# Gate tables of a product-key expert layer from bf16 one-hots, with the gate in three exact bf16 parts

## The chip, the cores and the metric

The kernel runs on one core of a Trainium2 chip. The metric is the device time of one execution in microseconds. Of the kernel before, three timed executions are at hand, and one more that was profiled.

## The reference

One layer of a streaming encoder on 512 tokens of width 2048, in f32: a mixer of two attention branches, then a PEER layer (retrieval of single-neuron experts by product keys), then a norm. Only the PEER layer matters here:

```python
scores = jnp.einsum('thpc,hpnc->thpn', q, sub_keys)        # 8 heads, 2 halves, 128 keys each
s1, i1 = lax.top_k(scores[:, :, 0], 16)
s2, i2 = lax.top_k(scores[:, :, 1], 16)
cand_score = s1[..., :, None] + s2[..., None, :]           # 256 candidates a head
cand_id = i1[..., :, None] * 128 + i2[..., None, :]
top_score, pos = lax.top_k(cand_score, 16)                 # over the 256
gates = jax.nn.softmax(top_score, axis=-1)
act = gelu(einsum('thkd,td->thk', expert_u[ids], x))
out = einsum('thk,thkd->td', gates * act, expert_v[ids])
```

Each token picks 8 x 16 = 128 of 16,384 experts. An expert's number is a pair (a, b) of two indices from 0 to 127.

## The kernel before

For the first 352 tokens the kernel doesn't gather experts. It multiplies with all 16,384 of them and weighs the result by a **gate table**: for each token a matrix of 128 x 128, which holds the gates at the 128 chosen pairs (a, b) and zero elsewhere. The other 160 tokens are served by gathering rows of the expert matrices.

The work on the PEER layer stands in this order in the program:

- *Selection* (`choose`): queries, scores, and top 16 by instructions of VectorE. It leaves three tiles: `ia` and `ib`, the two indices of each pick, and `gt`, its gate, all f32, with tokens on partitions.
- *Tables* (lines 766 to 793): `ia`, `ib` and `gt` are transposed by TensorE (`pstr`) and copied back by ScalarE, so that the 128 picks stand on the partitions and the tokens along the row. Then 22 blocks (`tb`) of 16 tokens follow, each in four groups of four tokens, 88 groups in all. VectorE makes one-hots for a group: one `tensor_tensor` compares `ib`, held for 128 elements, with the numbers 0 to 127 (`i128`) for four tokens at once, 512 elements (line 782, tile `ab`). Four `tensor_scalar` instructions, one for each token, compare `ia` with them and multiply by the gate (line 787). TensorE multiplies the two one-hots of a token, which sums over the 128 picks and gives the token's table in PSUM (`psgt`, line 789), ScalarE copies the four tables to `st` (line 790), and GpSimd's queue stores a block's tables to memory (`gsp`, line 791).
- *Weighted products* (`weigh` and after): 128 groups of experts, each with its up-projection (`psu`), the table's factors loaded from `gsp`, and the down-projection (`psy`).

`early` puts up-projections (`expert_up`) between the steps of selection and tables, one for two blocks of three. Such an up-projection is 48 products of 128 x 352 on TensorE (`psu`, lines 116 to 118), whose weights are loaded in two halves (`wr`), rounded by ScalarE (`wh`, line 108) and completed by VectorE (`wl`, line 109), and an activation (`gl`, line 536 on VectorE, 539 on ScalarE). `pace` puts gathers between them: GpSimd fetches 128 rows (`row`, line 561) and VectorE multiplies and sums 2048 elements (line 568).

Products with f32 operands (`psgt`) are single instructions that the trace shows as two records. The up- and down-projections use f32 values split into two parts of a type that TensorE takes in one pass.

Every engine works off its queue in order. The order within a queue is made by a scheduler that reorders what the program lists, by its own costs and by the data that instructions wait for. Each tag of a pool has a fixed number of buffers: `ab` two for each of the one-hots, `pg` (PSUM, `psgt`) two, `st` two, `wh` and `wl` three each.

## Time and profile before

| | us |
|---|---|
| median of three runs | 3785.46 |
| lowest and highest | 3780.77, 3790.85 |
| the profiled execution | 3782.03 |
| its span, from the first to the last instruction | 3780.3 |

The profiled execution has 1.7 us around its span. The tables are made from 1909 to 2118 us of the span. The page gives shares of busy time over the whole span; the windows view gives them for a stretch; the view of groups sums instructions of one line and shape; the timeline has single instructions with their start and duration. Instructions of one engine that follow each other overlap a little, so that the distance between starts is shorter than the duration.

### The profile page before, as it was taken

Reading aid. Unit: us, or ns where it says so; the run is one execution under the profiler, and the core shown is the slowest. Engines: PE = TensorE matmul, PEld = TensorE weight load, DVE = VectorE, ACT = ScalarE, POOL = GpSimd, SP = SyncE. Lnnn points to the kernel's source line nnn. Section 1 sums busy time; section 2 is a strip of 40 time slices with the busy share of each in tenths; the row PEclk is TensorE's granted clock in tenths of the full one; section 3 lists DMA queues with packets and bytes.
Section 4 is the critical chain, followed back from the end, with each engine's and each line's share of the span. In section 5 each row is a group of like instructions: output and inputs, shape, how many; then the busy total and the mean of one; then the engine's idle time right before and its main releaser. Section 6 shows DMA issues by size and latency. Waiting matters only on the chain.

```text
span 3780.3 us, 52236 instructions
## 1 busy us (share of the span) xinstructions
PE 3676.0 (97%) x20745; PEld 3384.4 (90%) x20745; DVE 2640.2 (70%) x4067; ACT 1291.3 (34%) x1808; POOL 515.2 (14%) x432
## 2 busy tenths in 40 slices
PE   8999999999999999999999898999999999999997
PEld 7888888888887878799999798999999999999997
DVE  5333445444555346799699888988888888888885
ACT  4334222232223223344355332333333333333333
POOL 0000000000000000011211122222222222222220
PEclk9999999999999999999999999999999999999999
DMA  4222222222224233376867899998999989999983
GB/s 141 80 78 77 98 95 95 89 87 84 85 95 138 95 100 101 128 267 251 294 229 264 288 336 333 352 334 326 333 336 348 345 324 349 340 343 344 332 306 112
DMA packets 233701, 827.26 MB, mean 219 GB/s; under 512 B 21736, under 2 KB 82664, under 8 KB 189680
## 3 DMA queue, kind: packets, MB, share of 16 engines
q1 hardware_dynamic: 174032, 450.30, 34.5%
q0 software_dynamic: 49920, 360.74, 24.8%
q10 hardware_dynamic: 9504, 12.88, 0.9%
q8 instruction: 163, 2.67, 0.3%
q14 instruction: 82, 0.67, 0.1%
HBM read 784.72 MB, written 39.11 MB: 218 GB/s over the span
## 4 chain that ended last, share of the span: by engine, by line
PE 81%; DVE 9%; DMA 5%; issue 3%; ACT 1%; SPq 0%; POOL 0%; DVEq 0%; POOLq 0%; ACTq 0%
PE psy L118 7%; PE psy L117 7%; PE psy L116 7%; PE psu L118 6%; PE psu L116 6%; PE psu L117 6%; PE psg L118 3%; PE psg L117 3%; PE psq L118 3%; PE psg L116 3%; PE psq L117 3%; PE psq L116 3%; DVE wl L109 2%; DVE ab L787 2%; PE psk L118 2%
## 5 line engine op out<-in xcount | busy, mean ns | idle before, releaser
L108 ACT ACTIVATE wh<-wr 128x1024 fp32r<-128x1024 f32 x768 | 813.6, 1061 | 1933.4 <-PE psy L117 581.0
L109 DVE TENSOR_TENSOR wl<-wr,wh 128x1024 fp32r<-128x1024 f32 x768 | 935.5, 1221 | 504.4 <-ACT wh L108 500.5
L116 PE MATMUL psy<-wg,wh 128*128 128x352 f32 x2048 | 668.6, 327 | 26.6 <-ACT wg L820 25.8
L117 PE MATMUL psy<-wg,wh 128*128 128x352 f32 x2048 | 672.0, 328 | 8.7 <-DVE wg L821 8.7
L118 PE MATMUL psu<-h,wl 128*128 128x352 f32 x2048 | 666.7, 326 | 12.8 <-DVE wl L109 12.5
L118 PE MATMUL psy<-wg,wl 128*128 128x352 f32 x2048 | 669.8, 328 | 8.4 <-DVE wl L109 8.3
L116 PE MATMUL psu<-h,wh 128*128 128x352 f32 x2048 | 666.6, 325 | 4.0 <-DVE gl L536 2.9
L117 PE MATMUL psu<-h,wh 128*128 128x352 f32 x2048 | 662.8, 324 | 0.0
L116 PEld LDWEIGHTS psy<-wg,wh 128*128 128x128 f32 x2048 | 391.1, 191 | 29.0 <-ACT wg L820 27.6
L118 PEld LDWEIGHTS psu<-h,wl 128*128 128x128 f32 x2048 | 385.5, 188 | 18.9 <-DVE wl L109 18.7
L117 PEld LDWEIGHTS psy<-wg,wh 128*128 128x128 f32 x2048 | 391.0, 191 | 11.0 <-DVE wg L821 10.9
L118 PEld LDWEIGHTS psy<-wg,wl 128*128 128x128 f32 x2048 | 391.0, 191 | 10.0 <-DVE wl L109 9.9
L116 PEld LDWEIGHTS psu<-h,wh 128*128 128x128 f32 x2048 | 386.6, 189 | 5.0 <-issue 3.2
L117 PEld LDWEIGHTS psu<-h,wh 128*128 128x128 f32 x2048 | 386.9, 189 | 0.0
L561 POOL DMA_INDIRECT row<-eu,idx x128 | 192.4, 1503 | 901.5 <-DVE row L568 606.4
L568 DVE SCALAR_TENSOR_TENSOR row<-row,rstd_t,h2g 128x2048 f32<-128x2048 f32 x128 | 300.1, 2345 | 6.5 <-DMA row<-eu,idx 6.5
L586 DVE SCALAR_TENSOR_TENSOR acc<-row,gact,acc 128x2048 f32<-128x2048 f32 x128 | 300.1, 2345 | 1.9 <-DMA row<-ev,idx 1.9
L561 POOL DMA_INDIRECT row<-ev,idx x128 | 182.2, 1424 | 508.0 <-DVE acc L586 478.1
L116 PE MATMUL psq<-h,wh 128*128 128x512 f32 x512 | 204.5, 399 | 8.8 <-ACT wh L108 8.8
L117 PE MATMUL psq<-h,wh 128*128 128x512 f32 x512 | 205.6, 401 | 1.5 <-DVE h L167 1.4
L118 PE MATMUL psq<-h,wl 128*128 128x512 f32 x512 | 204.6, 400 | 0.1
L118 PE MATMUL psg<-h,wl 128*128 128x512 f32 x512 | 203.3, 397 | 0.0
(311 smaller groups left out, 5513.7 us busy)
## 6 DMA issues: line engine op xcount, KB each, us to landing
wr<-uT SPq DMA_DIRECT2D x256, 512.0 KB
wr<-vP SPq DMA_DIRECT2D x256, 512.0 KB
wr<-w_qk SPq DMA_DIRECT2D x64, 512.0 KB
wr<-w_g SPq DMA_DIRECT2D x64, 512.0 KB
gsp<-st POOLq DMA_DIRECT2D x22, 1024.0 KB
wr<-w_br SPq DMA_DIRECT2D x32, 512.0 KB
wr<-w_o SPq DMA_DIRECT2D x32, 512.0 KB
wr<-w_q SPq DMA_DIRECT2D x32, 512.0 KB
```

The source lines that it names most:

```text
L108: nc.scalar.activation(hi, raw, AF.Copy)
L109: ins = nc.vector.tensor_tensor(lo, raw, hi.bitcast(F32), op=ALU.subtract)
L116: nc.tensor.matmul(ps, wh, ah, start=start, stop=False)
L117: nc.tensor.matmul(ps, wh, al, start=False, stop=False)
L118: nc.tensor.matmul(ps, wl, ah, start=False, stop=stop)
L561: nc.gpsimd.indirect_dma_start(out=row.rearrange("p k q -> p (k q)"), out_offset=None, in_=table, in_offset=bass.IndirectOffsetOnAxis(ap=i ...
L568: nc.vector.scalar_tensor_tensor(row, row, rstd_t[:, NT - 1:NT], h2g, op0=ALU.mult, op1=ALU.mult, accum_out=gact[:, i:i + 1])
L586: nc.vector.scalar_tensor_tensor(accg, row, gact[:, i:i + 1], accg, op0=ALU.mult, op1=ALU.add)
L787: nc.vector.tensor_scalar(ab[0][:, i], i128, tr[0][:, t:t + 1], tr[2][:, t:t + 1], op0=ALU.is_equal, op1=ALU.mult)
```

## The change

`ia` and `ib` become the halves of one tile, `iab`. After the transposes they are written as bf16, into the start of the same tile (`tid`; numbers up to 127 are exact in bf16). The gate is taken apart: its bf16 rounding, the bf16 rounding of the rest, and what then is left, each exact in bf16 (`tg`, three casts and two subtractions on VectorE).

For a group of four tokens one `tensor_tensor` makes the one-hots of both indices, 2 x 4 x 128 elements in bf16 (`eq`), and another multiplies the first index's one-hots by the three parts of the gate, 3 x 4 x 128 elements in bf16 (`ga`). TensorE then makes three bf16 products for a token, summed in PSUM. In the selection stage the two position tiles and the row of numbers that they are compared with become bf16 as well.

```diff
-        ia = s1p.tile([P, NT, HK], F32, name="ia")
-        ib = s1p.tile([P, NT, HK], F32, name="ib")
+        iab = s1p.tile([P, 2, NT, HK], F32, name="iab")
+        ia, ib = iab[:, 0], iab[:, 1]
...
-        i128 = s1p.tile([P, NK], F32, name="i128")
+        i128 = s1p.tile([P, NK], BF16, name="i128")
...
+            pa16, pb16 = small(BF16, "b0h"), small(BF16, "b2h")
-            nc.vector.tensor_tensor(pa_, pa_, pc_, op=ALU.add)
+            nc.vector.tensor_tensor(pa16, pa_, pc_, op=ALU.add)
...
+        packed = iab.rearrange("p n t q -> p (n t q)").bitcast(BF16)[:, :5 * ND * P].rearrange("p (n q) -> p n q", n=5)
+        tid, tg = packed[:, :2], packed[:, 2:]
         for n, src in enumerate((ia, ib, gt)):
             ps = psx.tile([P, ND, P], F32, tag="psx", name="pstr")
             for t in range(ND):
                 nc.tensor.transpose(ps[:, t], src[:, t], ident)
-            nc.scalar.activation(src[:, :ND], ps, AF.Copy)
-            tr.append(src.rearrange("p t q -> p (t q)"))
+            nc.scalar.activation((tid[:, n] if n < 2 else src[:, :ND].rearrange("p t q -> p (t q)")),
+                                 ps.rearrange("p t q -> p (t q)"), AF.Copy)
+        rest = gt[:, :ND].rearrange("p t q -> p (t q)")
+        for m in range(3):
+            nc.vector.tensor_copy(tg[:, m], rest)
+            if m < 2:
+                nc.vector.tensor_tensor(rest, rest, tg[:, m], op=ALU.subtract)
...
-                ab = [se.tile([P, 4, NK], F32, tag=f"ab{i}", bufs=2, name="ab") for i in range(2)]
-                nc.vector.tensor_tensor(ab[1], i128.unsqueeze(1).to_broadcast([P, 4, NK]),
-                                        tr[1][:, tk].unsqueeze(2).to_broadcast([P, 4, NK]), op=ALU.is_equal)
+                eq = se.tile([P, 2, 4, NK], BF16, tag="eq", bufs=2, name="eq2")
+                nc.vector.tensor_tensor(eq, i128.unsqueeze(1).unsqueeze(1).to_broadcast([P, 2, 4, NK]),
+                                        tid[:, :, tk].unsqueeze(3).to_broadcast([P, 2, 4, NK]), op=ALU.is_equal)
+                ga = se.tile([P, 3, 4, NK], BF16, tag="ga", bufs=2, name="ga")
+                nc.vector.tensor_tensor(ga, eq[:, 0].unsqueeze(1).to_broadcast([P, 3, 4, NK]),
+                                        tg[:, :, tk].unsqueeze(3).to_broadcast([P, 3, 4, NK]), op=ALU.mult)
                 ps = pg.tile([P, 4, NK], F32, tag="pg", name="psgt")
                 for i in range(4):
-                    t = tb * TB + t4 + i
-                    nc.vector.tensor_scalar(ab[0][:, i], i128, tr[0][:, t:t + 1], tr[2][:, t:t + 1], op0=ALU.is_equal,
-                                            op1=ALU.mult)
-                    nc.tensor.matmul(ps[:, i], ab[0][:, i], ab[1][:, i], start=True, stop=True)
+                    for m in range(3):
+                        nc.tensor.matmul(ps[:, i], ga[:, m, i], eq[:, 1, i], start=m == 0, stop=m == 2)
```

On VectorE's queue the first groups stand so in the kernel before (`ab` are the one-hots, `row` a gathered row, `gl` an up-projection's activation):

```order
L536 TENSOR_TENSOR gl<-psu,rstd 128x352
L568 SCALAR_TENSOR_TENSOR row,gact<-row,rstd_t,h2g 128x2048
L782 TENSOR_TENSOR ab<-i_9669,ib 128x512
L787 TENSOR_SCALAR ab<-i_9669,ia,gt 128x128 x4
L782 TENSOR_TENSOR ab<-i_9669,ib 128x512
L787 TENSOR_SCALAR ab<-i_9669,ia,gt 128x128 x4
```

And so in the changed kernel, from the parts of the gate on:

```order
L782 TENSOR_TENSOR gt<-gt,iab 128x384
L536 TENSOR_TENSOR gl<-psu,rstd 128x352
L780 CAST iab<-gt 128x384
L109 TENSOR_TENSOR wl<-wr,wh 128x1024
L791 TENSOR_TENSOR ga<-eq_15124,iab 128x1536
L791 TENSOR_TENSOR ga<-eq_15142,iab 128x1536
L788 TENSOR_TENSOR eq_15160<-i_9668,iab 128x1024
L788 TENSOR_TENSOR eq_15178<-i_9668,iab 128x1024
L791 TENSOR_TENSOR ga<-eq_15160,iab 128x1536
L791 TENSOR_TENSOR ga<-eq_15178,iab 128x1536
```

Two groups now go together, both comparisons and then both products, where before a group was finished before the next one began; the subtraction and cast of the gate's parts stand ahead of the first product, with a weight split between.

On TensorE's queue, where the tables begin, before (`psgt` are the tables, `psu` an up-projection):

```order
L789 MATMUL psgt<-ab 128x128 x4
L116 MATMUL psu<-h_8494,wh 128x352
L117 MATMUL psu<-h_8494,wh 128x352
L118 MATMUL psu<-h_8494,wl 128x352
L116 MATMUL psu<-h_8494,wh 128x352
L789 MATMUL psgt<-ab 128x128 x4
L117 MATMUL psu<-h_8494,wh 128x352
L118 MATMUL psu<-h_8494,wl 128x352
L116 MATMUL psu<-h_8494,wh 128x352
L117 MATMUL psu<-h_8494,wh 128x352
L789 MATMUL psgt<-ab 128x128 x2
```

And in the changed kernel, at the end of the first group's twelve products (each with its own load of weights, which the order now lists):

```order
L796 LDWEIGHTS ga
L796 MATMUL psgt<-eq_15124,ga 128x128
L117 MATMUL psu<-h_8494,wh 128x352
L118 MATMUL psu<-h_8494,wl 128x352
L116 MATMUL psu<-h_8494,wh 128x352
L117 MATMUL psu<-h_8494,wh 128x352
L118 MATMUL psu<-h_8494,wl 128x352
L116 MATMUL psu<-h_8494,wh 128x352
L796 LDWEIGHTS ga
L796 MATMUL psgt<-eq_15142,ga 128x128
```

A token's one product became three, and the up-projections moved: before, 654 of their products stand between the first and the last table, in 36 places four of them in a row and in two places 46; now 593 stand there, eight times 46 and six times 22 in a row, and up to ten groups of tables follow each other with none between. From the transposes to the down-projection it is 665 in both.

On SyncE's queue the weight loads keep their order; at the end of the stage the first load of the tables stands one weight load earlier. On GpSimd's queue the stores of tables and the gathers stand in a slightly different order.

## Rows read from the trace of the kernel before

**Rows 1.** The page, busy us (share of the span) and instructions of each engine.

```profile
PE 3676.0 (97%) x20745; PEld 3384.4 (90%) x20745; DVE 2640.2 (70%) x4067; ACT 1291.3 (34%) x1808; POOL 515.2 (14%) x432
```

**Rows 2.** Windows: stretch, its length, busy us by engine, granted clock, DMA share, GB/s.

```profile
1909.00:2118.00 209.00, 195.55 (x1371) 188.41 (x1369) 208.44 (x507) 122.72 (x131) 26.86 (x33) 0.99 0.71 258
2118.00:2129.10 11.10, 0.08 (x1) 0.00 (x0) 0.05 (x1) 1.02 (x1) 1.53 (x2) 0.65 0.87 310
```

**Rows 3.** The chain of waits, 1850 to 2220 us: start, us, what.

```profile
2026.27 1.03 DVE ab L787 x4
...
2119.43 5.83 DMA gsp<-st
2125.38 3.65 DMA h<-gsp
```

**Rows 4.** Groups, 1909.5 to 2118 us: count, busy us, mean ns, idle before.

```profile
L789 PE MATMUL psgt<-ab 128*128 128x128 f32 x704 | 98.6, 283 | 7.7 <-DVE ab L787 7.3 <-issue 0.5
L787 DVE TENSOR_SCALAR ab<-i,ia,gt 128x128 f32<-128x128 f32 x352 | 97.7, 343 | 0.0
...
L782 DVE TENSOR_TENSOR ab<-i,ib 128x512 f32<-128x512 f32 x88 | 60.2, 684 | 0.0
...
L109 DVE TENSOR_TENSOR wl<-wr,wh 128x1024 fp32r<-128x1024 f32 x29 | 35.0, 1216 | 0.0
...
L568 DVE SCALAR_TENSOR_TENSOR row<-row,rstd_t,h2g 128x2048 f32<-128x2048 f32 x12 | 28.1, 2344 | 0.0
...
L536 DVE TENSOR_TENSOR gl<-psu,rstd 128x352 f32<-128x352 f32 x14 | 7.3, 520 | 0.3 <-PE psu L118 0.2
```

**Rows 5.** Waits, 1909.5 to 2118 us: us in total, times, longest us.

```profile
PE psgt L789 <- DVE ab L787: 7.3, 11, 2.1
```

**Rows 6.** Timeline of VectorE, two places: start, us, engine, line, tiles.

```profile
1909.58 0.69 DVE L782 TENSOR_TENSOR ab<-i,ib 128x512 f32<-128x512 f32 x1
1910.19 1.11 DVE L787 TENSOR_SCALAR ab<-i,ia,gt 128x128 f32<-128x128 f32 x4
1911.21 0.68 DVE L782 TENSOR_TENSOR ab<-i,ib 128x512 f32<-128x512 f32 x1
...
1930.69 2.34 DVE L568 SCALAR_TENSOR_TENSOR row<-row,rstd_t,h2g 128x2048 f32<-128x2048 f32 x1
...
1932.96 1.21 DVE L109 TENSOR_TENSOR wl<-wr,wh 128x1024 fp32r<-128x1024 f32 x1
1934.10 0.68 DVE L782 TENSOR_TENSOR ab<-i,ib 128x512 f32<-128x512 f32 x1
```

**Rows 7.** Groups of VectorE in the selection stage, 1380 to 1900 us.

```profile
L700 DVE TENSOR_TENSOR eq<-b,i 128x512 bf16<-128x512 f32 x32 | 20.8, 683 | 0.0
...
L704 DVE TENSOR_TENSOR eq<-eq,f 128x512 bf16<-128x512 bf16 x32 | 12.4, 414 | 0.0
...
L705 DVE TENSOR_REDUCE ib<-eq 128x32 f32<-128x512 bf16 x16 | 10.7, 672 | 0.0
...
L748 DVE COPY spread<-ident 128x128 f32<-128x128 f32 x1 | 0.2, 218 | 0.0
```

**Rows 8.** Timeline of TensorE, 1954 to 1962 us.

```profile
1955.72 0.32 PE L118 MATMUL psu<-h,wl 128*128 128x352 f32 x1
1955.88 1.95 PE L789 MATMUL psgt<-ab 128*128 128x128 f32 x16
1957.58 0.41 PE L118 MATMUL psu<-h,wl 128*128 128x352 f32 x1
```

**Rows 9.** Windows of 4 us behind the last tables; the clock stands ahead of DMA's share.

```profile
2108.00:2112.00 4.00, 4.00 (x31) 4.00 (x31) 3.85 (x5) 1.56 (x3) 0.00 (x0) 1.00 0.94 362
...
2124.00:2128.00 4.00, 0.00 (x0) 0.00 (x0) 0.00 (x0) 0.00 (x0) 0.00 (x0) 0.50 0.91 330
...
2132.00:2136.00 4.00, 4.00 (x18) 4.00 (x18) 3.03 (x7) 1.99 (x4) 0.00 (x0) 0.61 0.65 190
2136.00:2140.00 4.00, 3.15 (x19) 2.77 (x19) 1.86 (x4) 1.03 (x2) 0.00 (x0) 1.00 0.51 151
```

More of the change, by code (lines that the diff above doesn't have):

```diff
@@ L633, in block_kernel @@
         pg = pool("pg", 2, space=PSUM, cm=s1)
-        ia = s1p.tile([P, NT, HK], F32, name="ia")
-        ib = s1p.tile([P, NT, HK], F32, name="ib")
+        iab = s1p.tile([P, 2, NT, HK], F32, name="iab")
+        ia, ib = iab[:, 0], iab[:, 1]
         gt = s1p.tile([P, NT, HK], F32, name="gt")
-        i16 = s1p.tile([P, TOPK], F32, name="i16")
+        i16 = s1p.tile([P, TOPK], BF16, name="i16")
         nc.gpsimd.iota(i16, pattern=[[1, TOPK]], base=0, channel_multiplier=0, allow_small_or_imprecise_dtypes=True)
-        i128 = s1p.tile([P, NK], F32, name="i128")
+        i128 = s1p.tile([P, NK], BF16, name="i128")
         nc.gpsimd.iota(i128, pattern=[[1, NK]], base=0, channel_multiplier=0, allow_small_or_imprecise_dtypes=True)
@@ L694, in choose @@
             nc.vector.tensor_tensor(pc_, pc_, lt, op=ALU.mult)
-            nc.vector.tensor_tensor(pa_, pa_, pc_, op=ALU.add)
+            pa16, pb16 = small(BF16, "b0h"), small(BF16, "b2h")
+            nc.vector.tensor_tensor(pa16, pa_, pc_, op=ALU.add)
             nc.vector.tensor_tensor(pd_, pd_, lt, op=ALU.mult)
-            nc.vector.tensor_tensor(pb_, pb_, pd_, op=ALU.subtract)
-            for (uf, f, dst) in ((pa_, ids[0], ia), (pb_, ids[1], ib)):
+            nc.vector.tensor_tensor(pb16, pb_, pd_, op=ALU.subtract)
+            for (uf, f, dst) in ((pa16, ids[0], ia), (pb16, ids[1], ib)):
                 eq = se.tile([P, n * TOPK, TOPK], BF16, tag="ab0", name="eq")
@@ L765, in block_kernel @@
             early(UPS, pace)
-        tr = []
+        s2.close()
+        se = pool("scat", 2, cm=s1)
+        packed = iab.rearrange("p n t q -> p (n t q)").bitcast(BF16)[:, :5 * ND * P].rearrange("p (n q) -> p n q", n=5)
+        tid, tg = packed[:, :2], packed[:, 2:]
         for n, src in enumerate((ia, ib, gt)):
@@ L771, in block_kernel @@
                 nc.tensor.transpose(ps[:, t], src[:, t], ident)
-            nc.scalar.activation(src[:, :ND], ps, AF.Copy)
-            tr.append(src.rearrange("p t q -> p (t q)"))
-        s2.close()
-        se = pool("scat", 2, cm=s1)
+            nc.scalar.activation((tid[:, n] if n < 2 else src[:, :ND].rearrange("p t q -> p (t q)")),
[5 more added lines that the diff above has]
+                nc.vector.tensor_tensor(rest, rest, tg[:, m], op=ALU.subtract)
         for tb in range(TD // TB):
```

## The prediction

> **What bounds the kernel now.** I read the page's busy shares first: TensorE is busy for 97% of the span [rows 1], so at first sight only TensorE work is worth taking out. The change, though, lies in one stage, and a stage has to be read alone. The windows view of that stage, 1909 to 2118 us, turns the picture round: VectorE is busy 208.44 of 209.00 us and TensorE 195.55 [rows 2]. The chain of waits agrees: inside the stage its pieces are the VectorE instructions of the table builder (`ab`), with the splits of weights (`wl`) and the gathered rows between them [rows 3]. TensorE waits there for the one-hots, 7.3 us in all in 11 places [rows 5]; VectorE waits for practically nobody. So what this stage is worth is read from VectorE, and TensorE time taken out of it is worth nothing as long as VectorE stays the longer of the two.
>
> The stage is a sum of VectorE steps, where a step is the distance from one start to the next (shorter than a duration, since neighbours overlap). A group of four tokens is one comparison of 512 elements, 0.61 us, and four scalar instructions, 1.02 us: 1.63 us [rows 6]. 88 groups make 143 us. Beside them run 29 weight splits of 1024 elements at 1.14 us, 12 gathered rows of 2048 at 2.27 us [rows 4, 6], and 14 activations of 352 elements, for which I estimate 0.45 us: 33 + 27 + 6 us. Together 210 us, against 208.44 us read. The sum closes, so it may be used for the changed kernel.
>
> **What the change takes out of VectorE's queue and puts in.** Out go 88 comparisons and 352 scalar instructions. In come 88 comparisons of 1024 elements (both indices at once) and 88 products of 1536 elements (three parts of the gate). The changed kernel thus has two instructions instead of five in a group, but each token now has 256 + 384 = 640 elements written by two-operand instructions instead of 128 by such and 128 by scalar ones. The question is at what rate they run.
>
> The step of a two-operand instruction is proportional to its elements: 0.61 us at 512, 1.14 at 1024, 2.27 at 2048 [rows 6], about 1.1 ns an element plus some 0.07 us, with every operand f32. I call this the single rate. At it the new comparison takes 1.14 us and the new product, halfway between 1.14 and 2.27, 1.70 us: 2.84 us a group, 1.21 us more than now.
>
> The new instructions have only bf16 operands, and the trace has one such two-operand instruction: the product in the selection stage, 414 ns for 512 elements, where the comparison ahead of it with f32 inputs takes 683 [rows 7]. The 269 ns between them are half of 512 elements' time. At that doubled rate the steps would be 0.60 and 0.87 us, 1.47 us a group, 0.16 us less than now. These are the two ends, and they have different signs.
>
> I take the slow end, for the shape of the operands. In the fast row all operands run on from element to element; its repeated factor is repeated by whole rows of 16. Both new instructions have one operand that stands still within a row: one index, or one part of a gate, is held for 128 elements. The rows nearest in this respect are the comparison that the change removes, and the bf16-writing comparison of the selection stage, 683 ns, in which an index is held for 16 elements: both at the single rate, though with f32 inputs [rows 4, 7]. That bf16 operands alone don't double a rate is shown by the reduction, 672 ns for 512 bf16 elements [rows 7]. No row has the held operand and bf16 together.
>
> Here the Trainium skill speaks against the change. Its "Vector Engine (DVE) Microarchitecture Reference", section 5.1 Performance modes, says that the paired 2-byte rate asks for a step of one element in every input and output, and that a two-source instruction with 2-byte operands which reads one element 16 times over was tried on trn2 and ran at the single rate, while a whole row read again and again kept the double one. No row here shows the first case; the second agrees with the 414 ns. By this page the sum is that of the slow end; by its "VectorE: DVE Perf Modes", tier table, read without the condition, a bf16 `tensor_tensor` gets the double rate, and the sum would be that of the fast end.
>
> So: 88 x 1.21 = **+106.5 us**, all on the path, since VectorE is what the stage waits for. At 1.675 us for the product (512 and 1024 drawn on) it would be 104.
>
> **The split of the gate.** Three casts and two subtractions of 384 elements go into VectorE's queue before the first product, once. A copy of 128 elements takes 218 ns [rows 7], a two-operand instruction of 512 takes 0.61 us: between 1.1 and 3.1 us. I take **+2 us**. The order puts a weight split and a gathered row among them, so that their chain of results doesn't leave the engine idle. The three transposes and their copies on ScalarE stay as they are in number and size.
>
> **TensorE.** 352 f32 products, which the trace shows as 704 records of 106 ns step (16 in 1.70 us [rows 8]), go out: 75 us. 1056 bf16 products of 128 columns come in. No bf16 product is in the trace. From below, 128 of the 352 columns of a one-pass product, which follows the next at 0.16 us [rows 8], are 0.058 us; from above, a bf16 pass is as long as one f32 record, 0.106 us. That makes 61 to 112 us. With the 665 expert products that the order has between the transposes and the down-projection, 0.16 us each or 107 us, TensorE has 168 to 219 us of work in a stage in which VectorE has some 318. It is hidden either way, and the 14 us gained at the lower end buy nothing.
>
> **The order.** Before, most expert products stand in twos to fours between two groups. Now they stand in blocks, eight of 46 among them, and the groups between them follow each other without cover. While TensorE works off a block of 46, 7.4 us, and then the next group, VectorE can build two groups ahead (two buffers of `eq2` and `ga`), 5.7 us, and the splits and rows that stand in between, 1.14 and 2.27 us. So a block costs VectorE nothing or up to some 2 us: 0 to 16 us in all. TensorE's clock can add to this. Where TensorE ran out of work at the end of the stage, the granted clock fell from 1.00 to 0.50, its lower level of 1.2 GHz, and was back at 1.00 some 5 us after the work had begun again [rows 9]. In the changed stage TensorE is busy for hardly more than half, so it may meet a block at the lower level and lose another 2 us or so there. I take **+2 us** for both, and 0 to 35 as the bounds, near the lower end because a split or a row stands at most of these places.
>
> ScalarE (122.72 us busy of 209 [rows 2]) has the same evictions. On SyncE the weight loads keep their order except at the end of the stage, where one load of the tables moves ahead of a weight load. On GpSimd the stores of tables and the gathers change places by one or two; the gathers are paced by VectorE's steps and have more time. What comes after, the last store and the load of the tables [rows 3], which VectorE and TensorE wait for in 2118 to 2129 us [rows 2], stays; I price it at nothing. At worst the store finds a quieter queue and gives back a few us of its 5.83.
>
> **The rivals.**
> *A, forecast: held operands run at the single rate.* +106.5 + 2 + 2 = +110.5 us. The profiled execution's 3782.03 us becomes 3892.5; the median shown, 3785.46, lies 3.4 us above it, so 3896 us. Its bounds: from below 104 + 1.1, less 6 for the store, less half the spread of the runs shown (5), 3880 us; from above 106.5 + 3.1 + 16, 3911.
> *B, the other side: bf16 doubles both instructions, as in the selection's product.* Place: the same queue. Price: 88 x -0.16 = -14, +2 for the split: -12 us, 3773 us. VectorE has then 198 us and TensorE 168 to 219. It decides only if the blocks cost nothing; the run ahead is then just 2.9 us against 7.4 us and a group, so that each of the eight blocks can take back 3 to 5 us, which ends at +12 to +28 and more if a bf16 pass takes 0.106 us. B reaches from 3773 to 3830 us. For it: the 414 ns row. Against it: the held operand.
> *C: TensorE's order and clock come out in front within A.* Place: the blocks of 46 and the groups behind them. With 0.106 us a pass and the lower clock at the head of each block, up to +35 us in place of A's 2, and more if the clock stays down: 3911 to 3960. For it: rows 9 and the blocks in the order. Against it: VectorE's surplus of 100 us.
>
> **How the numbers follow.** A has 0.80: every row with a held operand is at the single rate. C has 0.11. B has 0.09, since no row excludes it: 0.03 for faster by over 0.3% (11 us, about what a measurement of this kernel can tell from no change), 0.01 for within, 0.05 for slower. So faster 0.03, same 0.01, slower 0.96. The range 3880 to 3930 takes in A and the lower half of C; B is left out.
>
> **What would show it.** In the profile of the changed kernel the comparison of 1024 elements should last about 1.2 us and the product of 1536 about 1.75; 0.68 and 0.95 would mean B. The stage should be some 315 us long instead of 209, with VectorE busy in all of it, TensorE in hardly 60%, and the wait of the table's products for `ga` the longest of TensorE. If VectorE waits there for TensorE by more than 10 us, the order costs more than I gave it (C). Everything before the first comparison and after the load of the tables should last as long as before. The forecast is wrong if the stage grows by clearly more or less than 1.21 us a group.

## The result and the profile after

| | before | after |
|---|---|---|
| median, us | 3783.11 | 3907.91 |
| lowest and highest of 4 runs | 3778.07, 3790.85 | 3905.34, 3913.28 |
| the profiled execution | 3782.03 | 3906.15 |
| its span | 3780.3 | 3904.4 |

The changed kernel is slower: the ratio of the times is 1.0321, with a 95% interval of 1.0305 to 1.0337 (the quotient of the two medians is 1.0330, inside the interval). The medians stand 124.8 us apart, the two profiled executions 124.1.

The page, as in [rows 1], with its line of the granted clock in 40 slices of the span:

```profile
PE 3703.2 (95%) x21097; PEld 3399.9 (87%) x21097; DVE 2746.9 (70%) x3808; ACT 1292.1 (33%) x1808; POOL 516.5 (13%) x432
PEclk9999999999999999999977789999999999999999
```

VectorE's share of the span has not moved, 70%, although it works 107 us more; one stage holds all of that. And there is a dent in the clock, in the slices of the table stage. The windows of that stage, which answer to [rows 2], and two stretches of 20 us out of it (length, busy us of TensorE, its weight loads, VectorE, ScalarE and GpSimd, granted clock, DMA share, GB/s):

```profile
1909.00:2242.00 333.00, 224.06 (x1716) 204.27 (x1715) 313.76 (x246) 123.28 (x129) 31.37 (x33) 0.76 0.45 160
...
1940.00:1960.00 20.00, 9.49 (x75) 7.70 (x74) 19.09 (x15) 7.55 (x8) 1.08 (x2) 0.50 0.28 114
...
2120.00:2140.00 20.00, 17.10 (x132) 15.91 (x130) 17.00 (x15) 9.18 (x11) 2.27 (x2) 0.91 0.51 190
```

The stage is 333 us long where it was 209. VectorE is still what it waits for, but no longer without a gap: 313.76 of 333.00 us. TensorE's granted clock, 0.99 in this stage before, is 0.76 in the mean and 0.50, its lower level of 1.2 GHz, in the whole of 1940 to 1960 us. The groups that answer to [rows 4], 1908.6 to 2255.6 us (VectorE) and 1905 to 2245 us (TensorE):

```profile
L791 DVE TENSOR_TENSOR ga<-eq,iab 128x1536 bf16<-128x1536 bf16 x88 | 150.7, 1749 | 0.0
L788 DVE TENSOR_TENSOR eq<-i,iab 128x1024 bf16<-128x1024 bf16 x88 | 105.2, 1218 | 7.1 <-PE psgt L796 7.1
L109 DVE TENSOR_TENSOR wl<-wr,wh 128x1024 fp32r<-128x1024 f32 x29 | 34.8, 1216 | 0.0
L568 DVE SCALAR_TENSOR_TENSOR row<-row,rstd_t,h2g 128x2048 f32<-128x2048 f32 x12 | 28.1, 2343 | 0.0
L536 DVE TENSOR_TENSOR gl<-psu,rstd 128x352 f32<-128x352 f32 x14 | 7.3, 521 | 12.2 <-PE psu L118 12.2
```

```profile
L796 PE MATMUL psgt<-eq,ga 128*128 128x128 bf16 x1056 | 103.2, 271 | 103.1 <-DVE ga L791 102.9
```

The comparison of 1024 bf16 elements lasts 1218 ns, as long as the weight split of 1024 f32 elements below it, 1216. The product lasts 1749 ns. Splits, rows and activations have the counts of before, 29, 12 and 14. The last two columns are the news: VectorE now waits 7.1 us for the buffers of the comparison and 12.2 us for the up-projections, where it waited 0.3 us before.

The timeline of VectorE shows how the groups go, two at a time (start, duration, engine, line, tiles, in brackets the idle time before):

```profile
1926.70 2.35 DVE L788 TENSOR_TENSOR eq<-i,iab 128x1024 bf16<-128x1024 bf16 x2
1928.97 3.42 DVE L791 TENSOR_TENSOR ga<-eq,iab 128x1536 bf16<-128x1536 bf16 x2
1932.31 1.22 DVE L788 TENSOR_TENSOR eq<-i,iab 128x1024 bf16<-128x1024 bf16 x1
1933.94 1.23 DVE L788 TENSOR_TENSOR eq<-i,iab 128x1024 bf16<-128x1024 bf16 x1 [0.42 <-PE psgt L796]
1935.09 3.42 DVE L791 TENSOR_TENSOR ga<-eq,iab 128x1536 bf16<-128x1536 bf16 x2
...
2232.50 0.52 DVE L536 TENSOR_TENSOR gl<-psu,rstd 128x352 f32<-128x352 f32 x1 [2.15 <-PE psu L118]
```

The steps are (1928.97 - 1926.70) / 2 = 1.14 us for a comparison and (1932.31 - 1928.97) / 2 = 1.67 us for a product: 2.81 us a group against 1.63 before. The timeline of TensorE at the same place, and in one of the blocks of 46 expert products:

```profile
1926.84 0.84 PE L796 MATMUL psgt<-eq,ga 128*128 128x128 bf16 x12 [0.82 <-DVE ga L791]
1930.78 1.46 PE L796 MATMUL psgt<-eq,ga 128*128 128x128 bf16 x12 [3.09 <-DVE ga L791]
1932.44 1.46 PE L796 MATMUL psgt<-eq,ga 128*128 128x128 bf16 x12 [0.21 <-DVE ga L791]
...
1984.79 1.51 PE L796 MATMUL psgt<-eq,ga 128*128 128x128 bf16 x24
1986.11 0.41 PE L116 MATMUL psu<-h,wh 128*128 128x352 f32 x1
...
2113.72 0.64 PE L118 MATMUL psu<-h,wl 128*128 128x352 f32 x1
...
2117.09 0.49 PE L117 MATMUL psu<-h,wh 128*128 128x352 f32 x1
2117.39 0.49 PE L118 MATMUL psu<-h,wl 128*128 128x352 f32 x1
...
2119.22 0.32 PE L118 MATMUL psu<-h,wl 128*128 128x352 f32 x1
2119.38 0.32 PE L116 MATMUL psu<-h,wh 128*128 128x352 f32 x1
```

A group's twelve products take 0.84 us until TensorE has stood idle for 3.09 us; from there on they take 1.46. And a block of 46 begins with products at a step of 0.29 to 0.30 us (2117.39 - 2117.09) and ends with the usual 0.16 (2119.38 - 2119.22).

Behind the stage the chain is that of [rows 3], a store of tables and their load:

```profile
2243.78 8.07 DMA gsp<-st
2251.96 3.51 DMA h<-gsp
```

VectorE waits there 12.3 us where it waited 11.3.

### The profile page after: what moved, and what is told of

It is laid out like the page before. It is cut to its first block, busy times and chain, and to the rows that moved or that the text cites. A ratio compares the mean times of both kernels' runs of the same rounds, so it can differ in the third digit from the quotient of the medians.

```text
span 3904.4 us, 52682 instructions
## 1 busy us (share of the span) xinstructions
PE 3703.2 (95%) x21097; PEld 3399.9 (87%) x21097; DVE 2746.9 (70%) x3808; ACT 1292.1 (33%) x1808; POOL 516.5 (13%) x432
## 4 chain that ended last, share of the span: by engine, by line
PE 79%; DVE 9%; issue 5%; DMA 5%; ACT 1%; POOL 1%; SPq 0%; DVEq 0%; POOLq 0%; ACTq 0%
PE psy L118 7%; PE psy L117 7%; PE psy L116 7%; PE psu L118 6%; PE psu L116 6%; PE psu L117 6%; PE psg L118 3%; PE psg L117 3%; PE psq L118 3%; PE psg L116 3%; PE psq L117 3%; PE psq L116 3%; DVE ga L791 2%; PE psk L118 2%; PE psb L118 2%
## 5 line engine op out<-in xcount | busy, mean ns | idle before, releaser
L109 DVE TENSOR_TENSOR wl<-wr,wh 128x1024 fp32r<-128x1024 f32 x768 | 934.8, 1220 | 504.9 <-ACT wh L108 501.6
L116 PEld LDWEIGHTS psy<-wg,wh 128*128 128x128 f32 x2048 | 390.5, 191 | 30.3 <-ACT wg L827 29.0
L116 PEld LDWEIGHTS psu<-h,wh 128*128 128x128 f32 x2048 | 391.7, 191 | 6.8 <-issue 3.6
L117 PEld LDWEIGHTS psu<-h,wh 128*128 128x128 f32 x2048 | 391.2, 191 | 0.0
```

The costliest lines, as they stand in the source:

```text
L109: ins = nc.vector.tensor_tensor(lo, raw, hi.bitcast(F32), op=ALU.subtract)
L116: nc.tensor.matmul(ps, wh, ah, start=start, stop=False)
L117: nc.tensor.matmul(ps, wh, al, start=False, stop=False)
```

## The experiments

All ratios are to the kernel before, timed beside the experiment on the same chip (3784.39 us for the first four, 3786.67 for the next two, 3784.11 for the last two). The quotients of the medians differ from these ratios by at most 0.0007.

**Theory and rivals.** The theory: the held operand keeps VectorE at the single rate, which is 104 us of the 124; and the rest comes from TensorE's order and clock, which make VectorE wait. Against the first half: bf16 comparisons and products of this size might run at the single rate for another reason. Against the second: the three passes for each token might be too much work for TensorE.

### No operand is held: tokens innermost

The one-hots are laid out with the four tokens of a group innermost. An index or a gate part then runs on from token to token, and the numbers 0 to 127 are written four times each beforehand.

```diff
-                eq = se.tile([P, 2, 4, NK], BF16, ...)
-                nc.vector.tensor_tensor(eq, i128.unsqueeze(1).unsqueeze(1).to_broadcast([P, 2, 4, NK]),
-                                        tid[:, :, tk].unsqueeze(3).to_broadcast([P, 2, 4, NK]), op=ALU.is_equal)
+                eq = se.tile([P, 2, NK, 4], BF16, ...)
+                nc.vector.tensor_tensor(eq, i128t.unsqueeze(1).to_broadcast([P, 2, NK, 4]),
+                                        tid[:, :, tk].unsqueeze(2).to_broadcast([P, 2, NK, 4]), op=ALU.is_equal)
...
-                        nc.tensor.matmul(ps[:, i], ga[:, m, i], eq[:, 1, i], start=m == 0, stop=m == 2)
+                        nc.tensor.matmul(ps[:, i], ga[:, m, :, i], eq[:, 1, :, i], start=m == 0, stop=m == 2)
```

> Edit to the changed kernel: the one-hots are laid out with the four tokens innermost, so that no operand of the two VectorE instructions stands still from element to element (the numbers 0 to 127 are written out four times each; an index or gate part runs over its four tokens and is repeated by whole rows of four). Same elements, same types, same three products. Theory H (the held operand forbids the double rate): the comparison of 1024 falls from 1.22 to about 0.68 us, the product of 1536 from 1.75 to about 0.95, a group from 2.81 to 1.47 us of VectorE, the stage from 333 to about 200 us, the whole to 3765 to 3785 us. Rival S (these instructions run at the single rate for another reason: the comparison itself, bf16 of this size, repeated operands of any kind): durations stay, 3890 to 3910 us. TensorE's operands are then read 8 bytes apart; if that is slow its products show it (more than 0.65 us for twelve at the full clock), and the gain is smaller.

Measured: 3813.1 us, ratio 1.0069 (1.0052 to 1.0086). The groups of VectorE, and two rows of TensorE's timeline:

```profile
L793 DVE TENSOR_TENSOR ga<-eq,iab 128x1536 bf16<-128x1536 bf16 x88 | 83.8, 954 | 1.3
...
L790 DVE TENSOR_TENSOR eq<-gt,iab 128x1024 bf16<-128x1024 bf16 x88 | 60.7, 691 | 31.3 <-PE psgt L798 30.3
```

```profile
1930.69 1.58 PE L798 MATMUL psgt<-eq,ga 128*128 128x128 bf16 x12
1932.02 0.41 PE L116 MATMUL psu<-h,wh 128*128 128x352 f32 x1
```

The window of most of its stage, with the granted clock as the third number from the end:

```profile
1920.00:2100.00 180.00, 180.00 (x1303) 171.40 (x1302) 146.60 (x175) 91.28 (x95) 20.84 (x23) 1.00 0.65 229
```

The durations are those of the doubled rate, 691 and 954 ns instead of 1218 and 1749, for the same elements, operations and types. So the held operand is the cause of VectorE's rate. The total missed its expectation, for a reason that lies elsewhere: TensorE now reads both operands of the table products 8 bytes apart, and twelve of them take 1932.02 - 1930.69 = 1.33 us, at a granted clock of 1.00, where the changed kernel needs half of that. TensorE, busy in all 180 us of that window, becomes the bound, and VectorE waits 30.3 us for it.

### The change without bf16 and without the split

From the kernel before: both indices compared at once, the gate multiplied in place, all in f32, one product for a token.

```diff
+                eq = se.tile([P, 2, 4, NK], F32, tag="eq", bufs=2, name="eq2")
+                nc.vector.tensor_tensor(eq, i128..., tid[:, :, tk]..., op=ALU.is_equal)
+                ga = eq[:, 0]
+                nc.vector.tensor_tensor(ga, ga, tr[2][:, tk].unsqueeze(2).to_broadcast([P, 4, NK]), op=ALU.mult)
...
+                    nc.tensor.matmul(ps[:, i], ga[:, i], eq[:, 1, i], start=True, stop=True)
```

> Edit to the kernel before: both indices compared at once (1024 elements) as in the change, but in f32, and the gate in one f32 part (a product of 512 elements in place of four scalar instructions), one f32 product for a token. Theory H (an element costs the same in f32 and in bf16 as long as an operand is held; the price is the number of elements): 1.14 + 0.61 = 1.75 us a group instead of 1.63, 88 x 0.12 = +10.6 us on the kernel before, about 3794 us. Rival (two indices at once is itself dear, or the scalar instructions were): more than 25 us from the kernel before in either direction.

Measured: 3808.8 us, ratio 1.0071 (1.0054 to 1.0088). VectorE's groups, and its timeline in a tail of 14 groups that stand without expert products between them:

```profile
L783 DVE TENSOR_TENSOR eq<-i,iab 128x1024 f32<-128x1024 f32 x88 | 104.2, 1220 | 10.6 <-PE psgt L789 10.5
L786 DVE TENSOR_TENSOR eq<-eq,gt 128x512 f32<-128x512 f32 x88 | 56.6, 684 | 0.0
```

```profile
2119.15 1.22 DVE L783 TENSOR_TENSOR eq<-i,iab 128x1024 f32<-128x1024 f32 x1 [1.63 <-PE psgt L789]
2120.85 1.23 DVE L783 TENSOR_TENSOR eq<-i,iab 128x1024 f32<-128x1024 f32 x1 [0.48 <-PE psgt L789]
```

The f32 comparison of 1024 elements takes 1220 ns, the bf16 one of the changed kernel 1218: bf16 with a held operand buys nothing. The loss of 24.4 us against the kernel before is more than the 10.6 expected, and just under the 25 us that the rival named; 10.5 us of it are such waits for pairs of groups, at a clock of 0.80 and then 0.59 in the windows of 20 us from 2100 on. These are waits in pairs as in the changed kernel; of the rest, some 3 us, the cause stays open.

### One pass instead of three

The second and third part of the gate are made, but not multiplied: this kernel's tables hold the gate's first part only.

```diff
-                    for m in range(3):
-                        nc.tensor.matmul(ps[:, i], ga[:, m, i], eq[:, 1, i], start=m == 0, stop=m == 2)
+                    nc.tensor.matmul(ps[:, i], ga[:, 0, i], eq[:, 1, i], start=True, stop=True)
```

> Edit to the changed kernel: VectorE makes all three parts of the gate, TensorE multiplies only the first (the second and third are left out of the tables). VectorE's work is the same; TensorE has 4 products a group instead of 12, and the order keeps its blocks of 46 up-projection products. Theory (VectorE's elements set the stage; what it waits for TensorE is a group's products at the lower clock, 1.46 us, and blocks entered at the lower clock): the 7 us of waits of the comparisons for the tables' products go, the 14 us of waits for the up-projections stay, 3895 to 3905 us. Rival (the three passes set the pace): the stage loses 2/3 of the passes, 700 of 0.054 us or more, 38 us and more, below 3875 us.

Measured: 3905.15 us, ratio 1.0321 (1.0302 to 1.034), the changed kernel's own. VectorE's waits from 1908.6 to 2250 us (us in total, times, longest):

```profile
DVE gl L536 <- PE psu L118: 20.2, 12, 2.3
```

The window of its stage:

```profile
1909.00:2243.00 334.00, 180.75 (x1024) 157.79 (x1023) 313.81 (x247) 124.15 (x134) 31.86 (x33) 0.71 0.45 162
```

The waits for the comparison's buffers are gone, and those behind the blocks of expert products, which were expected to stay, have grown from 12.2 to 20.2 us; the one makes up for the other. The blocks stand as in the changed kernel (in two places a block of 22 and one of 4 have become one of 26), but the granted clock is lower, 0.71, and a block of 46 takes 8.8 to 10.3 us. Two thirds of TensorE's table work can go without a gain that could be measured: the three passes are not what VectorE waits for.

### TensorE filled with work for nothing

Sixteen products more for each group, into a tile that nobody reads.

```diff
+                pd = psx.tile([P, 4, P], F32, tag="psx", name="pdum")
+                for i in range(16):
+                    nc.tensor.matmul(pd[:, i % 4], ga[:, 0, i % 4], eq[:, 1, i % 4], start=True, stop=True)
```

> Edit to the changed kernel: behind each group's twelve products TensorE makes sixteen more of the same size, whose result nobody reads: 1408 of 0.054 us, 76 us more of TensorE work in the stage. By the order the up-projections then stand in small portions between the groups (8 to 23 products) and not in blocks of 46. Theory C (VectorE's 21 us of waits come from TensorE's lower clock and its blocks, not from its amount of work): the granted clock in the stage rises towards 1.00, the waits of VectorE fall below 8 us, and the kernel with more work is faster, 3885 to 3900 us. Rival W (TensorE's work is what VectorE waits for): the waits grow by 20 us and more, 3925 us or above.

Measured: 3890.74 us, ratio 1.0278 (1.0261 to 1.0295): 17 us faster than the changed kernel, with some 76 us more work on TensorE. The window of its stage, and VectorE's waits in it:

```profile
1909.00:2227.00 318.00, 261.86 (x3104) 242.90 (x3102) 316.44 (x248) 127.10 (x131) 36.77 (x33) 0.99 0.49 174
```

```profile
DVE eq L788 <- PE pdum L799: 0.3, 1, 0.3
```

The granted clock is 0.99 where it was 0.76, VectorE is busy in 316.44 of 318 us, and what remains over the kernel before, 106.3 us, is nearly the term of VectorE's elements and the gate's split alone (103.8 + 1.8, below). But the extra products have also moved the others: the expert products now stand in portions of 8 to 23 between single groups, with a tail of 40 groups behind them. Clock and order had changed together, which the last two experiments were to take apart.

### Pairs of tokens innermost

As in the first experiment, with two tokens innermost instead of four; TensorE reads 4 bytes apart.

```diff
-                eq = se.tile([P, 2, 4, NK], BF16, ...)
+                eq = se.tile([P, 4, NK, 2], BF16, ...)
...
-                ga = se.tile([P, 3, 4, NK], BF16, ...)
+                ga = se.tile([P, 2, 3, NK, 2], BF16, ...)
...
+                        nc.tensor.matmul(ps[:, i], ga[:, i // 2, m, :, i % 2], eq[:, 2 + i // 2, :, i % 2],
+                                         start=m == 0, stop=m == 2)
```

> The changed kernel with its one-hots laid out in pairs of tokens, [.., 128, 2]: no operand stands still any more, as in the run with four tokens innermost, but TensorE now reads its bf16 operands 4 bytes apart instead of 8. Theory H (a held operand alone kept VectorE at the single rate, and TensorE reads elements 4 bytes apart at full rate, as it does f32 ones): comparison about 0.69 us, product about 0.95 us, 1.47 us a group (129 us for 88 groups against 247); twelve products of TensorE in about 0.65 us as in the changed kernel; stage 196 to 215 us, total 3768 to 3790 us, level with the kernel before or a little faster. Rival S (any step above 2 bytes halves TensorE's rate): twelve products in 1.3 us, TensorE bounds the stage, 3805 to 3815 us as with four tokens innermost.

Measured: 3774.1 us, ratio 0.9963 (0.9949 to 0.9978). VectorE's groups, TensorE's timeline, and the windows of the stage up to the last expert product and behind it:

```profile
L799 DVE TENSOR_TENSOR ga<-eq,iab 128x1536 bf16<-128x1536 bf16 x88 | 83.7, 953 | 1.3
...
L795 DVE TENSOR_TENSOR eq<-gt,iab 128x1024 bf16<-128x1024 bf16 x88 | 59.9, 683 | 0.0
```

```profile
1929.90 0.86 PE L806 MATMUL psgt<-eq,ga 128*128 128x128 bf16 x12
1930.58 0.41 PE L118 MATMUL psu<-h,wl 128*128 128x352 f32 x1
```

```profile
1909.00:2066.00 157.00, 156.27 (x1403) 146.46 (x1401) 156.11 (x193) 98.08 (x106) 22.93 (x25) 1.00 0.81 291
2066.00:2113.00 47.00, 25.48 (x331) 20.55 (x332) 45.69 (x58) 29.54 (x29) 5.19 (x8) 0.93 0.56 217
```

Both engines run at their full rate: the comparison and the product as in the first experiment, and twelve products in 1930.58 - 1929.90 = 0.68 us. VectorE is busy in nearly all of the stage again, which ends at 2113 us where it ended at 2118. This version computes what the changed kernel computes, with the gate in all three parts, and is 12.6 us faster than the kernel before: 0.4%, little, but its interval lies below 1.

### Pairs of tokens and two parts of the gate

The third part of the gate is left out, so the tables hold the gate to some 16 bits only.

```diff
-        for m in range(3):
+        for m in range(2):
...
-                ga = se.tile([P, 2, 3, NK, 2], BF16, ...)
+                ga = se.tile([P, 2, 2, NK, 2], BF16, ...)
```

> As the run with pairs of tokens innermost, with two parts of the gate instead of three (the third part, the last 8 bits of the gate, is left out): eight bf16 products in place of twelve in a group and a product of 1024 elements instead of 1536 on VectorE, 1.20 us a group there instead of 1.47. Theory H: VectorE has 24 us less than in the run with three parts, and TensorE 19 us less; 3745 to 3775 us, faster than the kernel before. Rival S (step above 2 bytes halves TensorE's rate): eight products at 0.11 us, 0.9 us a group, TensorE about 200 us in the stage, 3770 to 3790 us. Rival O (the order and the clock set the time, whichever engine has less work): no faster than the run with three parts by more than 5 us.

Measured: 3751.41 us, ratio 0.9905 (0.9888 to 0.9921). Its product of 1024 elements:

```profile
L799 DVE TENSOR_TENSOR ga<-eq,iab 128x1024 bf16<-128x1024 bf16 x88 | 56.6, 684 | 0.0
```

With 83.7 - 56.6 = 27 us less of the product's busy time (24 in steps), the kernel is 22.7 us faster. The stage follows VectorE's elements in the faster layout, too.

### The order alone

The changed kernel with the first part's product issued twice, 4 products a group more. The scheduler then spreads the expert products in portions of 4 to 18 between single groups and leaves a tail of 41 groups.

```diff
                 for i in range(4):
+                    for r in range(1):
+                        nc.tensor.matmul(ps[:, i], ga[:, 0, i], eq[:, 1, i], start=True, stop=True)
```

> The changed kernel with the first part's product of each token issued twice (the repeat starts the sum over again, the result is the same): 16 bf16 products a group in place of 12, about 19 us of TensorE time more in the stage, against 76 us in the run with idle time filled. With it the expert products no longer stand in blocks of 46 and 22 but in portions of 4 to 18 between single groups, with a tail of 41 groups that has none. Theory O (the order decides: VectorE waits only where TensorE, after some us of idle time and at the lower clock, meets a long block or two groups that follow each other closely): VectorE waits less than 4 us for TensorE instead of 20.9, total 3885 to 3895 us, as with idle time filled. Rival F (how full TensorE is decides, and 19 us are too little): waits of 15 us or more stay, total 3900 to 3912 us.

Measured: 3893.33 us, ratio 1.0285 (1.0261 to 1.0308). VectorE's waits from 1908.6 to 2228 us, and a window of the tail:

```profile
DVE gl L536 <- PE psu L118: 2.6, 3, 1.7
```

```profile
2140.00:2160.00 20.00, 12.70 (x110) 10.86 (x108) 19.76 (x15) 7.21 (x7) 0.53 (x1) 0.50 0.25 105
```

As expected if the order decides. VectorE waits 2.6 us instead of 19.3 (the 20.9 of the expectation, and the 13.8 in the next one, take in a wait of 1.7 us that ends at 1905.96 us, ahead of the first comparison). The mean clock of the stage is hardly higher than in the changed kernel, 0.78 against 0.76 (window 1909 to 2228), and 0.50 in all of the tail; there VectorE is busy for 19.76 of 20 us all the same. A low clock alone costs VectorE nothing, as long as groups come one by one and no block of expert products stands between them.

### The same order with slower products

The changed kernel in its own order, with the second operand of each table product read 8 bytes apart and the columns written back in their places.

```diff
-                        nc.tensor.matmul(ps[:, i], ga[:, m, i], eq[:, 1, i], start=m == 0, stop=m == 2)
+                        nc.tensor.matmul(ps[:, i].rearrange("p (a b) -> p b a", b=4), ga[:, m, i],
+                                         eq[:, 1, i].rearrange("p (a b) -> p b a", b=4), start=m == 0, stop=m == 2)
```

> The changed kernel in its own order, instruction by instruction, where each table product reads its second operand 8 bytes apart and writes its columns back in their places; the first operand, which is loaded as weights, is read as before. Same result, no instruction more. If reading the second operand 8 bytes apart is what halved TensorE's rate in the run with four tokens innermost, twelve products take 1.3 us at the full clock in place of 0.65, TensorE is busy some 57 us longer in the stage without more work, and blocks and pairs of groups stay where they are. Theory K (the blocks cost VectorE only because TensorE meets them at the lower clock): the granted clock is 1.00 in nearly all of the stage, the wait for up-projections (13.8 us) falls under 5, the pairs go on waiting 0.3 to 0.4 us each (7 us), total 3888 to 3900 us. Rival B (the blocks cost by their place, whatever the clock): the wait for up-projections stays at 12 us or more, total 3903 to 3915 us. If the clock stays low in spite of it, twelve products would take 2.6 us and pairs wait 1.5 us each: 3930 us or more. If the loaded operand is the one that matters, nothing changes: 3905 to 3912 us, twelve products in 0.65 us.

Measured: 3932.81 us, ratio 1.0387 (1.0365 to 1.0409), and VectorE's waits from 1908.6 to 2275 us:

```profile
DVE eq L788 <- PE psgt L796: 38.5, 51, 1.5
DVE gl L536 <- PE psu L118: 6.5, 6, 2.0
```

The window of its stage, and its table products in one place of it:

```profile
1909.00:2273.00 364.00, 276.85 (x1717) 260.57 (x1716) 318.08 (x246) 126.14 (x130) 32.12 (x33) 0.86 0.41 147
```

```profile
1997.03 2.95 PE L796 MATMUL psgt<-eq,ga 128*128 128x128 bf16 x24
1999.73 0.41 PE L116 MATMUL psu<-h,wh 128*128 128x352 f32 x1
```

This kernel was to hold the clock up without moving an instruction, and it did so only in part: 0.86 in the mean, 0.66 to 1.00 in the windows of 20 us from 1920 on. The total is the one expected for a clock that stays low in spite of it, 3930 us or more. The waits behind the blocks fell to half, 6.5 us against 12.2, which lies between what the two theories asked for and decides for neither, and the longer products cost 31 us more at the pairs. Its blocks of 46 took 7.5 to 7.9 us, nearly the 7.36 of the full clock, so little of what is left was lost inside them. The last one, with a wait of 2.00 us behind it, began 3.43 us behind the start of the splits ahead of it (2250.27 to 2253.70) where it was 1.35 in the changed kernel (2221.26 to 2222.61), since the 24 products before it took 4.96 us, 0.21 each: the halved rate at the lower clock. The kernel shows that the second operand's reading or the output's writing in steps halves TensorE's rate, too (24 products between 1997.03 and 1999.73 us, 0.11 each), not which of the two. What the blocks would cost at the full clock, in the changed kernel's own order, stays without a run of its own.

## Why the prediction held, and where it was off

The range was 3880 to 3930 us, and the time is 3907.9. For the profiled execution the forecast was 3892.5 us and the measurement is 3906.15, 13.6 us more. Step by step, from the first comparison to the load of the tables, where the changed kernel took 2255.50 - 1908.67 = 346.8 us and the kernel before 2129.05 - 1909.58 = 219.5:

| term | forecast, us | measured, us |
|---|---|---|
| elements of VectorE, 88 x (2.81 - 1.63) | 106.5 | 103.8 |
| split of the gate, 3 x 0.27 + 2 x 0.47 | 2 | 1.8 |
| waits of VectorE, 19.3 - 0.3 | 2 | 19.0 |
| ends that no next instruction overlaps, at 28 waits | 0 | 2 |
| wait for the store and load, 12.3 - 11.3 | 0 | 1.0 |

These make 127.6 us, against 127.4 read. The changed kernel reached the first comparison 0.9 us earlier and needed 2.4 us less from the load to its end, which leaves 124.1. So the forecast fell 20 us short in the waits (17, 2 and 1), and some 6 us came back where it had expected nothing: 2.7 because the product's step had been taken too long, 0.9 ahead of the stage and 2.4 behind it. That the miss is only 13.6 us is to that extent luck.

**The rate was right, and for its reason.** The choice between the two ends, 2.84 and 1.47 us a group, was made by the shape of the operands. The changed kernel shows 2.81, and with the held operand taken away 691 + 954 ns stand in place of 1218 + 1749. The kernel's own selection stage has the cleanest row, which answers to [rows 7]: the change turned both operands of the comparison there into bf16, one of them held for 16 elements, and its time did not move, 683 ns before:

```profile
L705 DVE TENSOR_TENSOR eq<-eq,f 128x512 bf16<-128x512 bf16 x32 | 12.4, 414 | 0.0
L701 DVE TENSOR_TENSOR eq<-b0h,i 128x512 bf16<-128x512 bf16 x16 | 10.9, 684 | 0.0
```

This is the case that the Trainium skill tells of in its "Vector Engine (DVE) Microarchitecture Reference", section 5.1 Performance modes, and of which no row of the kernel before could speak: one element read 16 times over, 2-byte operands, the single rate. The runs here agree, for 16 and for 128 repeats. One of the prediction's witnesses was weaker than it said: the reduction of 672 ns [rows 7] reads bf16 but writes f32, so it isn't an instruction with bf16 operands alone.

**The product's step** was taken as 1.70 us, halfway between two steps of f32; it is 1.67. The named alternative of 1.675, 104 us in all, was the better one. The line drawn through the steps, 1.1 ns an element and 0.07 us, doesn't meet its own rows (1.20 us at 1024 elements, where the row has 1.14); the sum didn't use it.

**TensorE's amount of work** was rightly given as hidden. A bf16 pass takes 0.055 us at the full clock (24 between 1984.79 and 1986.11 us), a little below the lower end of 0.058 to 0.106. At the lower clock it takes some 0.107, since twelve then last 1.46 us and not 0.84. With the slow expert products at the head of the blocks that is why TensorE is busy for 67% of the stage, where the prediction said hardly 60.

**The order and the clock are the step that failed**: 2 us taken, with bounds of 0 to 35, and 21 measured more than before (19 of waits, 2 of ends that nothing overlaps). The prediction had set 10 us of such waits as the point from which this rival comes out in front; in mechanism it did. The time stayed below the 3911 us at which this rival was to begin, and inside the range, which had been drawn to take in the lower half of it. Two things had been left out of the 2 us.

The first is the pair. The scheduler builds two groups together, and there are two buffers of `eq2`. The second comparison of a pair has to wait until the last twelve products of the pair before have been made. At the full clock these take 0.84 us, and VectorE doesn't notice (the pair at 1926.70). At the lower clock they take 1.46, and VectorE waits up to 0.42 us, 19 times: 7.1 us. The prediction had looked at what VectorE can build ahead, not at what it must get back.

The second is how often the clock is down. The prediction named the rows where it fell, at the end of the stage [rows 9], and allowed for a slow head of each block, but then let the splits and rows that stand there cover it. The timeline says otherwise. At 0.16 us a product a block of 46 takes 7.36 us; three of them took 9.51 (2113.72 to 2123.23), 9.69 (2222.61 to 2232.30) and 7.74 us (2162.03 to 2169.77), and the waits of VectorE right behind them were 1.97, 2.15 and 0.21 us. (It is the activation `gl` that waits, for the block's last product, and all that stands behind it in VectorE's queue.) All nine waits behind blocks go so: each is what the block took beyond 0.16 us a product, less 0.1 to 0.3 us. Four of them, 5.3 us of the 12.2, stand behind blocks of 22, which took 4.6 to 5.1 us instead of 3.52 and which the prediction had not priced. Three blocks of 46 took 7.75, 8.29 and 8.64 us, and `gl` did not wait: beside each of these a gathered row of 2.27 us stands in VectorE's queue (at 2206.20, 1976.28 and 2084.76 us). So by the trace the work ahead of `gl` covered just a block at full speed, and what the lower clock added was paid in full; a row does cover more, but rows stood at three such places and not at most.

That the waits need both, the order in pairs and blocks and the lower clock, is shown from one side by the run with the order spread (low clock in its tail, hardly any waits). On the other side three runs share the order of the blocks, nearly or wholly: at a mean clock of 0.71 (one pass), 0.76 (the changed kernel) and 0.86 (slower products) VectorE waited 20.2, 12.2 and 6.5 us behind them. The waits fall as the clock rises, but the table products differ too, so this supports the clock's part and doesn't single it out; the full clock in the unchanged order was not brought about by any run.

**After the stage** nothing was expected, and 2.4 us were given back between the load and the end, 1.0 us lost ahead of it. The store took 8.07 us instead of 5.83, so the quieter queue that the prediction allowed for did not come.

**The rival of the doubled rate** was real, only in another layout: its figure for VectorE, 1.47 us a group, is the step in the run with pairs of tokens innermost (0.60 and 0.87), and its time of 3773 us is what that run took, 3774.1. The fear that the blocks take back 12 us and more did not come true there: in that layout the scheduler made portions of 1 to 19 expert products and no block of 46 between the tables, and TensorE's clock stayed at 1.00 until the expert products were used up.

## What to carry to other kernels

Before a two-operand instruction is turned into bf16 for its rate, look whether any of its operands stands still within a row; if so, lay out the tile so that a pair of neighbours runs innermost, and look what the reader of the tile then pays for its step. Where an engine is given less work than the one it feeds, ask what clock it will have when a long block meets it, and whether the other engine must get buffers back from it. A stage is predicted from the queue that sets it, but the width of the range from how that queue and the next one are interleaved.

## What the runs showed of the hardware

- TensorE's rate depends on how far apart its operands' elements lie: twelve bf16 products of 128 columns take 0.66 us read in a row, 0.68 us read 4 bytes apart, and 1.33 us read 8 bytes apart, all at a granted clock of 1.00 and with both operands read alike. The Trainium skill, "SBUF — State Buffer", section Specifications (TRN2), asks for at least two hits to each 16-byte line for full bandwidth and says that each step to a new line costs something. Four elements a line, at 4 bytes, and two a line, at 8 bytes, both meet that condition. Here four kept the rate and two halved it, so two hits were not enough, and the measurement decides.
- Work for nothing made a kernel faster: 1408 products that nobody reads brought TensorE's clock in the stage from 0.76 to 0.99 and, with the other order that came with them, the time from 3907.9 to 3890.7 us.
- One product more for each token, 352 in all, let the scheduler spread the expert products otherwise, and the kernel with more work was 14.6 us faster than the one without (3893.33 against 3907.91 us). Its scheduled order weighed more than its work.
